# Later adaLN blocks in the first MLP, and attention's small TensorE pieces gathered

## The chip, the cores and the metric

One core of a Trainium2 chip runs the whole program. The metric is the device time of one execution in microseconds (us), median of three runs, lower being better. Five engines take part: TensorE (PE, matrix products and transposes), VectorE (DVE), ScalarE (ACT), GpSimd (POOL) and SyncE (SP, which issues the loads from DRAM). Each runs its own list of instructions in order, and waits where an operand or a buffer is not ready.

## The reference

A trunk of two layers over 256 tokens of width 1024, for one sequence. Layer 0 mixes tokens by a gated convolution, layer 1 by attention with 16 heads of 64; each is followed by an MLP of width 4096. Every sub-layer is modulated (shift, scale, gate) by a vector `c`: that is adaLN, six vectors of 1024 for each layer, each a product of `silu(c)` with a 1024 x 1024 piece of `ada_w`.

```
def reference(x, c, ...):
    cond = silu(c)
    for i in range(2):
        mod = cond @ ada_w[i] + ada_b[i]
        sh1, sc1, g1, sh2, sc2, g2 = split(mod, 6)
        h = rms_norm(x, mix_norm_g[i]) * (1 + sc1) + sh1
        y = conformer_conv(h, ...) if i == 0 else moba_attention(h, w_qkv, q_norm_g, k_norm_g, w_o)
        x = x + g1 * y
        h = rms_norm(x, mlp_norm_g[i]) * (1 + sc2) + sh2
        x = x + g2 * (square(relu(h @ mlp_w1[i])) @ mlp_w2[i])
    return x
```

With 256 tokens there is one key block, so the attention is plain causal attention: q and k are normalised over each head, scores get a slope times the distance, a softmax, and the product with v.

## The kernel before

**Products in three parts.** Every large product is done in fp32 accuracy as three matmuls: weights and activations are each cut into a high and a low part, and `mm3` (L207 to L211) issues high weight by high activation (L208), high weight by low activation (L209), and low weight by high activation (L210), 128 x 128 weights against 258 columns (256 tokens and one column for the shift). A block is 1 MB of weights, 1024 rows by 256 columns; it fills two PSUM banks of 24 matmuls each. The weights come from DRAM into a tile `raw` (five buffers, loaded by SP in the order in which the code asks). `split` (L190 to L203) makes the two parts in two halves: ACT casts the high part `wh` (L196), DVE subtracts for the low part `wl` (L199), and from the fourth block of the first MLP on POOL does a quarter of it (L201). In that MLP a half serves four of the eight matmul triples of both banks, so the third matmul of a bank is the first that needs `wl`.

**The first MLP.** `six` runs the first three w1 blocks (six banks) while the norm's factor is still being made; the factor `rs_ext` (L759, the "seam") is then written and each bank is drained by `evict` (DVE, `tx`, L797), two ACT functions (`s`, `sh`, L833 to L835) and a DVE subtraction (`sl`, L836). The w1 blocks b = 3 to 15 and 16 w2 blocks follow. Beside them, DVE works through adaLN blocks: `ada_dve` loads 1 MB of `ada_w` and issues four DVE operations of 128 x 512 (L299 for the first of a vector, L301 for the others), 24 such blocks in this MLP. `slots` is a list of 32 places: `fill()` takes the next one, three after `six`, one after each block b = 3 to 15, one after each w2 block. The first 8 adaLN blocks ("half 0") are needed first.

**Attention.** For four blocks of four heads (`Heads`, b = 0 to 3) PE's small pieces stand between the triples of the qkv products and, for the last, of the output product `ko`: sums of squares `st`, their transposition `stt`, `kb` (the norm factors of k spread, after DVE's chain from `vs` to `rb`, L961 to L966), `pvt` (v transposed), two `ss` (scores), two `pt` (probabilities transposed), two `po` (product with v). `plan(t)` puts them on a clock that counts the triples issued (`tick`, `at`): the table `ts` gives the offsets in the order squares, stats, norms, keys, values, (scores), (turn), (product). All small pieces take their PSUM from `aux`, three banks in rotation.

**Order.** PE's order is that of the code and the clock. The order of the other engines, and which of two ready instructions stands first, is set when the program is built, by a scheduler that knows `issue_after` (an instruction may be placed only behind the named one). SP's loads go in the order asked, each when a `raw` buffer is free.

Of the kernel before, what the change touches and what calls it, by code (L numbers as in the profile page):

```python
# [30 lines left out]
def trunk(ctx, tc, x, c, ada_w, ada_b, mix_g, mlp_g, w_in, b_in, dw, dw_b, ln_g, ln_b, w_out, b_out,  # L31
# [13 lines left out]
    def aux(name):  # L45
        return axp.tile([P, 512], F32, name=name, tag="ax")
# [4 lines left out]
    def mm_bank(name):  # L51
        return mmp.tile([P, 512], F32, name=name, tag="mm")
# [7 lines left out]
    def at(d, f):  # L60
        later.append((clock[0] + d, f))
# [8 lines left out]
    def drain():  # L70
        while later:
            tick()
# [15 lines left out]
    VEC, cols, box = {}, {}, {}  # L88
# [97 lines left out]
    def load(src, into=None):  # L186
        r = raw() if into is None else into
        box["load"] = sy.dma_start(r, src).ins
        return r

    def split(r, pool_kt=3, parts=1):
        wh = wp.tile([P, 2048], F32R, name="wh")
        wl = wp.tile([P, 2048], F32R, name="wl")
        n = 2048 // parts
        for a in range(0, 2048, n):
            box["cut"] = [act.copy(wh[:, a:a + n], r[:, a:a + n]).ins]  # L196
            m = a + n - 256 * pool_kt
            if m > a:
                box["cut"].append(dve.tensor_sub(wl[:, a:m], r[:, a:m], wh[:, a:m].bitcast(F32)).ins)  # L199
            if pool_kt:  # L200
                pool.tensor_tensor(wl[:, m:a + n], r[:, m:a + n], wh[:, m:a + n].bitcast(F32), op=OP.subtract)  # L201
        return wh, wl

    def kmajor(src):
        return src.rearrange("(k p) n -> p k n", p=P)

    def mm3(ps, wh, wl, ah, al, start, stop, **kw):  # L207
        pe.matmul(ps, wh, ah, start=start, stop=False, **kw)  # L208
        pe.matmul(ps, wh, al, start=False, stop=False, **kw)  # L209
        pe.matmul(ps, wl, ah, start=False, stop=stop, **kw)  # L210
        tick()  # L211
# [247 lines left out]
    half = [b[:, j * S:(j + 1) * S] for b in banks for j in range(2)]  # L459
# [277 lines left out]
    def norm_shift(l, v):  # L737
        sh = mod[:, l, v, :]
        act.copy(xh[:, :, S], sh)
        dve.tensor_sub(xl[:, :, S], sh, xh[:, :, S].bitcast(F32))  # L740
# [55 lines left out]
    def evict(ps, t):  # L796
        box["evict"] = dve.tensor_mul(t, ps[:, :NE], rs_ext).ins  # L797
# [22 lines left out]
    def mlp(l, slots):  # L820

        def fill():
            for f in slots.pop(0) if slots else ():
                f()

        with tc.tile_pool(name=f"mlp{l}", bufs=1) as mp:
            sh = mp.tile([P, FF // P, S], F32R, name="sh")
            sl = mp.tile([P, FF // P, S], F32R, name="sl")
            def finish(ps, f):
                t = mp.tile([P, NE], F32, name="tx", bufs=3)  # L830
                evict(ps, t)
                s = mp.tile([P, S], F32, name="s2", bufs=4)
                act.activation(s, t[:, :S], AF.Relu, bias=t[:, S:S + 1])  # L833
                act.activation(sh[:, f, :], s, AF.Square)
                act.activation(s, s, AF.Square)  # L835
                dve.tensor_sub(sl[:, f, :], s, sh[:, f, :].bitcast(F32))  # L836

            def w1_split(b):
                return split(load(kmajor(w1[l, :, b * 256:(b + 1) * 256])), 1 if l == 0 and b >= 3 else 0, 2)

            six(w1_split, "m1", finish)
            with tc.issue_after(box["evict"]):
                for _ in range(3):
                    fill()
            for b in range(3, FF // 256):
                with tc.issue_after(box["seam"]) if b > 3 else ExitStack():
                    wh, wl = w1_split(b)
                for j in range(2):
                    f = 2 * b + j
                    ps = mm_bank("m1")  # L850
                    for k in range(KT):
                        o = 256 * k + P * j
                        mm3(ps[:, :NE], wh[:, o:o + P], wl[:, o:o + P], xh[:, k, :], xl[:, k, :],
                            start=(k == 0), stop=(k == KT - 1))
                    finish(ps, f)
                fill()
            def put_out(n):
                po = aux("ot")
                for t in range(2):
                    pe.transpose(po[:, t * P:(t + 1) * P], xT[:, n, t * P:(t + 1) * P], ident)  # L860
                o = mp.tile([P, S], F32, name="ot", bufs=2)
                act.copy(o, po[:, :S])
                sy.dma_start(out[0, :, n * P:(n + 1) * P].rearrange("(t p) n -> p t n", p=P),
                             o.rearrange("p (t n) -> p t n", t=2))
            if l == 0:
                acc = work.tile([P, S], F32, name="acc", bufs=2)
            for b in range(D // 256):
                ps = [mm_bank("m2") for _ in range(2)]
                for kc in range(4):
                    wh, wl = split(load(kmajor(w2[l, kc * D:(kc + 1) * D, b * 256:(b + 1) * 256])), 1 if l == 0 else 0, 2)  # L870
                    for j in range(2):
                        for k in range(KT):
                            o = 256 * k + P * j
                            kk = kc * KT + k
                            mm3(ps[j][:, :S], wh[:, o:o + P], wl[:, o:o + P], sh[:, kk, :], sl[:, kk, :],
                                start=(kk == 0), stop=(kk == FF // P - 1))
                        if kc < 3:
                            continue
                        n = 2 * b + j
                        dve.scalar_tensor_tensor(xT[:, n, :], ps[j][:, :S], mod[:, l, 5, n:n + 1],  # L880
                                                 xT[:, n, :], op0=OP.mult, op1=OP.add)
                        if l == 0:
                            norm_prep(1, 0, n, acc)
                        else:
                            at(12, lambda n=n: put_out(n))
                    fill()

            if l == 0:
                norm_shift(1, 0)
                norm_scale()  # L890
            else:
                drain()

    seq = [[(0, 5), (1, 1)], [(1, 0), (1, 2), (1, 4), (1, 3)]]
    slots = [[] for _ in range(32)]
    for half, vs in enumerate(seq):
        fs = [lambda l=l, v=v, q=q: ada_dve(l, v, q) for l, v in vs for q in range(4)]
        for n, f in enumerate(fs):
            slots[(1 if half == 0 else 15) + n * 15 // len(fs)].append(f)
    mlp(0, slots)  # L900


    with tc.tile_pool(name="attn", bufs=1) as ap:
# [14 lines left out]
        class Heads:  # L918
# [3 lines left out]
                self.b, self.tx, self.p, self.pT = b, {}, {}, {}  # L922

            def plan(self, t):
                ts = (2, 5, 11, 24, 26, (30, 40), (52, 70), (60, 78)) if self.b < 3 else (1, 11, 15, 27, 24, (31, 38), (47, 55), (55, 63))
                at(t + ts[0], self.squares)
                at(t + ts[1], self.stats)
                at(t + ts[2], self.norms)
                at(t + ts[3], self.keys)
                at(t + ts[4], self.values)  # L930
                for j in range(2):
                    at(t + ts[5][j], lambda j=j: self.scores(j))
                    at(t + ts[6][j], lambda j=j: self.turn(j))
                    at(t + ts[7][j], lambda j=j: self.product(j))
# [109 lines left out]
        for b in range(4):  # L1044
            hb = Heads(b)

            def take(ps, n):
                t = hb.tx[n // 2, n % 2] = ap.tile([P, NE], F32, name="tqkv", bufs=8)
                evict(ps, t)

            def qkv_split(z):
                return split(load(kmajor(w_qkv[0, :, z * D + b * 256:z * D + (b + 1) * 256])), 0, 2)

            if b == 0:
                six(qkv_split, "qkv", take)
                hb.plan(0)
            for z in range(3 if b == 0 else 0, 3):
                wh, wl = qkv_split(z)
                if z == 2:
                    hb.plan(7 if b < 3 else 0)  # L1060
                for j in range(2):
                    ps = mm_bank("qkv")
                    for k in range(KT):
                        o = 256 * k + P * j
                        mm3(ps[:, :NE], wh[:, o:o + P], wl[:, o:o + P], xh[:, k, :], xl[:, k, :],
                            start=(k == 0), stop=(k == KT - 1))
                    take(ps, 2 * z + j)
# [30 lines left out]
```

## Time and profile before

| | |
|---|---|
| time, median of three runs | 678.72 us (678.38 to 680.17) |
| the profiled execution's own time | 676.28 us |
| its span in the profile | 674.4 us |
| PE busy | 655.1 us, 97% |
| DVE busy | 494.5 us, 73% |
| ACT busy | 369.9 us, 55% |
| POOL busy | 125.3 us, 19% |
| data moved | 150.07 MB |

The span runs from the first to the last recorded instruction; the time has 1.9 us more around it. Matmuls overlap each other, so a busy PE shows rows of some 0.28 us whose starts are 0.12 us apart. In a timeline a row is a run of like instructions: start, length, engine, line, operation, what it writes and reads, shape and count, and in brackets the idle time ahead of it with what ended it. In this execution the first MLP's seam is at 172 us, its w1 blocks end near 257 us, its w2 blocks near 343 us, and attention's small pieces lie between 375 and 476 us.

### The profile page before, as it was taken

The page shows a single profiled execution, that of the slowest core. Times are in us where ns is not written, and L with a number is a line of the kernel's source. Part 1 is how long each engine was busy: PE and PEld are TensorE (multiplying, and loading weights), DVE is VectorE, ACT ScalarE, POOL GpSimd, SP SyncE. Part 2 cuts the span into 40 slices and gives each one's busy share as a digit, 9 for nine tenths or more (in the row PEclk, how much of TensorE's full clock was granted, in tenths as well). Part 3 has the DMA queues.
Part 4 walks back from the last instruction along what each step waited for, and adds up shares of the span by engine and source line. Part 5 has one row for each costly group of instructions (what it writes and reads, how often), then busy time and mean ns, then how long its engine had stood idle before and what let it go on. Part 6 is the DMA issues. An engine that isn't in the chain of part 4 may idle for free.

```text
span 674.4 us, 14400 instructions
## 1 busy us (share of the span) xinstructions
PE 655.1 (97%) x5909; PEld 607.0 (90%) x5909; DVE 494.5 (73%) x924; ACT 369.9 (55%) x678; POOL 125.3 (19%) x167
## 2 busy tenths in 40 slices
PE   7899999999979999999999899999999999999997
PEld 6777865699979999999999888888999999999997
DVE  3647993558999899999964888886878986444440
ACT  4437442485866667254443566575659777533330
POOL 5461042302523424344420000000200000000000
PEclk9999999999979999999999999999999999999999
DMA  8998509675589899999992723433266996555300
GB/s 304 340 351 299 220 8 370 237 252 201 188 275 319 281 302 311 358 340 368 339 322 96 239 75 126 136 119 123 68 197 236 312 304 194 172 189 178 119 18 16
DMA packets 107871, 150.07 MB, mean 223 GB/s; under 512 B 2871, under 2 KB 91120, under 8 KB 107806
## 3 DMA queue, kind: packets, MB, share of 16 engines
q1 hardware_dynamic: 107310, 149.04, 65.8%
q8 instruction: 46, 0.75, 0.4%
q14 instruction: 19, 0.16, 0.1%
q0 software_dynamic: 352, 0.07, 0.1%
q10 hardware_dynamic: 144, 0.06, 0.0%
HBM read 148.10 MB, written 1.05 MB: 221 GB/s over the span
## 4 chain that ended last, share of the span: by engine, by line
PE 86%; DVE 6%; POOL 2%; ACT 2%; DMA 2%; issue 1%; SPq 1%; DVEq 0%; ACTq 0%; POOLq 0%
PE m L208 18%; PE m L210 18%; PE m L209 17%; PE cv L403 3%; PE qkv L208 3%; PE qkv L209 3%; PE qkv L210 3%; PE ci L208 2%; PE ko L208 2%; PE ko L209 2%; PE ko L210 2%; PE rep L393 2%; PE ci L210 2%; PE ci L209 2%; DMA keep<-in_conv_w_in_dram 2%; DVE wl L199 1%
## 5 line engine op out<-in xcount | busy, mean ns | idle before, releaser
L199 DVE TENSOR_TENSOR wl<-raw,wh 128x1024 fp32r<-128x1024 f32 (+2 forms) x176 | 204.8, 1184 | 59.2 <-ACT wh L196 58.2
L196 ACT CAST wh<-raw 128x1024 fp32r<-128x1024 f32 x176 | 177.9, 1044 | 111.6 <-PE m L209 58.1
L210 PE MATMUL m<-xh,wl 128*128 128x258 f32 x512 | 145.4, 284 | 4.2 <-DVE wl L199 4.2
L208 PE MATMUL m<-xh,wh 128*128 128x258 f32 x512 | 146.1, 285 | 0.5 <-DVE xT L789 0.5
L209 PE MATMUL m<-xl,wh 128*128 128x258 f32 x512 | 145.6, 284 | 0.0
L208 PE MATMUL m<-sh,wh 128*128 128x256 f32 x512 | 145.4, 284 | 0.0
L210 PE MATMUL m<-sh,wl 128*128 128x256 f32 x512 | 144.1, 281 | 0.0
L209 PE MATMUL m<-sl,wh 128*128 128x256 f32 x512 | 144.0, 281 | 0.0
L210 PEld LDWEIGHTS m<-xh,wl 128*128 128x128 f32 x512 | 97.8, 191 | 4.4 <-DVE wl L199 4.4
L208 PEld LDWEIGHTS m<-xh,wh 128*128 128x128 f32 x512 | 97.6, 191 | 1.7 <-DVE xT L789 0.9
L208 PEld LDWEIGHTS m<-sh,wh 128*128 128x128 f32 x512 | 96.4, 188 | 1.6 <-issue 1.6
L209 PEld LDWEIGHTS m<-xl,wh 128*128 128x128 f32 x512 | 97.8, 191 | 0.0
L209 PEld LDWEIGHTS m<-sl,wh 128*128 128x128 f32 x512 | 96.4, 188 | 0.0
L210 PEld LDWEIGHTS m<-sh,wl 128*128 128x128 f32 x512 | 96.4, 188 | 0.0
L201 POOL TENSOR_TENSOR wl<-raw,wh 128x256 fp32r<-128x256 f32 (+1 forms) x60 | 68.5, 1153 | 108.6 <-ACT wh L196 106.0
L301 DVE SCALAR_TENSOR_TENSOR ada_a<-raw,cond,ada_a 128x512 f32<-128x512 f32 x98 | 81.2, 860 | 0.6 <-DMA raw<-in_ada_w_dram 0.4
L208 PE MATMUL qkv<-xh,wh 128*128 128x258 f32 x192 | 57.2, 298 | 0.0
L833 ACT ACTIVATE s<-tx 128x256 f32<-128x256 f32 x64 | 31.7, 506 | 41.1 <-DVE tx L797 41.1
L209 PE MATMUL qkv<-xl,wh 128*128 128x258 f32 x192 | 54.3, 283 | 0.0
L210 PE MATMUL qkv<-xh,wl 128*128 128x258 f32 x192 | 54.1, 282 | 0.0
L730 POOL TENSOR_TENSOR acc<-acc,nsq 128x256 f32<-128x256 f32 x15 | 12.8, 851 | 158.0 <-ACT nsq L728 157.4
L208 PEld LDWEIGHTS qkv<-xh,wh 128*128 128x128 f32 x192 | 36.2, 189 | 4.6 <-issue 4.6
(256 smaller groups left out, 1125.1 us busy)
## 6 DMA issues: line engine op xcount, KB each, us to landing
raw<-in_mlp_w_dram SPq DMA_DIRECT2D x64, 1024.0 KB, 6.5
raw<-in_ada_w_dram SPq DMA_DIRECT2D x46, 1024.0 KB, 7.5
raw<-in_attn_w_qkv_dram SPq DMA_DIRECT2D x12, 1024.0 KB, 5.5
keep<-in_conv_w_in_dram SPq DMA_DIRECT2D x8, 512.0 KB, 9.3
raw<-in_conv_w_in_dram SPq DMA_DIRECT2D x8, 512.0 KB, 5.3
raw<-in_conv_w_out_dram SPq DMA_DIRECT2D x4, 1024.0 KB, 8.4
raw<-in_attn_w_o_dram SPq DMA_DIRECT2D x4, 1024.0 KB, 4.9
early<-in_ada_w_dram SPq DMA_DIRECT2D x2, 1024.0 KB
```

Of the source, the lines that this page charges most:

```text
L196: box["cut"] = [act.copy(wh[:, a:a + n], r[:, a:a + n]).ins]
L199: box["cut"].append(dve.tensor_sub(wl[:, a:m], r[:, a:m], wh[:, a:m].bitcast(F32)).ins)
L201: pool.tensor_tensor(wl[:, m:a + n], r[:, m:a + n], wh[:, m:a + n].bitcast(F32), op=OP.subtract)
L208: pe.matmul(ps, wh, ah, start=start, stop=False, **kw)
L209: pe.matmul(ps, wh, al, start=False, stop=False, **kw)
L210: pe.matmul(ps, wl, ah, start=False, stop=stop, **kw)
L301: dve.scalar_tensor_tensor(a, w, cond[:, k, 0:1], a, op0=OP.mult, op1=OP.add)
L393: pe.matmul(ps[32 * r:32 * r + 32, :284], ident[:, 32 * g:32 * g + 32], UT[i][:, r:r + 284], start=True, stop=True, tile_position=(0, 32 * ...
L403: pe.matmul(ps[32 * g:32 * g + 32, :S], W[:, g, q, :], G[:, g, 4 * q:4 * q + S], start=(q == 0), stop=(q == 7), tile_position=(0, 32 * g))
L730: pool.tensor_tensor(acc, acc, q, op=OP.add)
L833: act.activation(s, t[:, :S], AF.Relu, bias=t[:, S:S + 1])
```

## The change

Two parts. The first moves half 0 of the adaLN blocks to later slots: from slots 1, 2, 4, 6, 8, 10, 12, 14 to slots 3, 4, 6, 7, 9, 10, 12, 13, and holds the slots behind blocks b = 3, 4 and 5 back behind the newest `evict`. The second replaces attention's table of offsets: the pieces of all four head blocks get new places. No operation is added or removed.

```diff
@@ mlp: the loop over w1 blocks
                     finish(ps, f)
-                fill()
+                with tc.issue_after(box["evict"]) if b < 6 else ExitStack():
+                    fill()
@@ slots of the first MLP
         for n, f in enumerate(fs):
-            slots[(1 if half == 0 else 15) + n * 15 // len(fs)].append(f)
+            slots[3 + n * 12 // len(fs) if half == 0 else 15 + n * 15 // len(fs)].append(f)
@@ Heads.plan
-                ts = (2, 5, 11, 24, 26, (30, 40), (52, 70), (60, 78)) if self.b < 3 else (1, 11, 15, 27, 24, (31, 38), (47, 55), (55, 63))
+                ts = ((2, 5, 12, 30, 42, (36, 42), (58, 66), (63, 75)),
+                      (9, 12, 18, 31, 47, (37, 47), (60, 79), (66, 85)),
+                      (9, 12, 18, 31, 47, (37, 47), (60, 79), (66, 85)),
+                      (1, 12, 18, 31, 43, (37, 43), (53, 59), (59, 64)))[self.b]
@@ the qkv loop
                 if z == 2:
-                    hb.plan(7 if b < 3 else 0)
+                    hb.plan(0)
```

In triples counted from the end of `six` in attention, the head blocks' clocks start at 0, 39, 87 and 128 before, and at 0, 32, 80 and 128 now. The 40 small pieces stand in 37 separate places between triples before, and in 26 now.

DVE's order from the seam on, before. `tx<-m_2175` drains a bank of the blocks that `six` ran, `tx<-m_2265` the first bank after them, `s_…` are ACT's outputs that `sl` needs, twelve `ada_a` operations in all stand ahead of the `wl` of block b = 5:

```order
L797 TENSOR_TENSOR tx<-m_2175,rs_ext 128x258
L299 TENSOR_SCALAR ada_a<-raw,cond 128x512 x2
L836 TENSOR_TENSOR sl<-s_2216,sh 128x256
L836 TENSOR_TENSOR sl<-s_2223,sh 128x256
L301 SCALAR_TENSOR_TENSOR ada_a<-raw,cond,ada_a 128x512 x2
L836 TENSOR_TENSOR sl<-s_2230,sh 128x256
L836 TENSOR_TENSOR sl<-s_2237,sh 128x256
L301 SCALAR_TENSOR_TENSOR ada_a<-raw,cond,ada_a 128x512 x4
L797 TENSOR_TENSOR tx<-m_2265,rs_ext 128x258
```

Ten rows on, behind four more `ada_a` operations, the two `wl` of block 5 follow. The same place now:

```order
L797 TENSOR_TENSOR tx<-m_2175,rs_ext 128x258
L836 TENSOR_TENSOR sl<-s_2216,sh 128x256
L836 TENSOR_TENSOR sl<-s_2223,sh 128x256
L797 TENSOR_TENSOR tx<-m_2252,rs_ext 128x258
L836 TENSOR_TENSOR sl<-s_2230,sh 128x256
L836 TENSOR_TENSOR sl<-s_2237,sh 128x256
L797 TENSOR_TENSOR tx<-m_2284,rs_ext 128x258
L299 TENSOR_SCALAR ada_a<-raw,cond 128x512 x2
L301 SCALAR_TENSOR_TENSOR ada_a<-raw,cond,ada_a 128x512
L836 TENSOR_TENSOR sl<-s_2279,sh 128x256
L301 SCALAR_TENSOR_TENSOR ada_a<-raw,cond,ada_a 128x512
L199 TENSOR_TENSOR wl<-raw,wh 128x768
```

Four adaLN operations instead of twelve stand ahead of block 5's first `wl`, and none ahead of the drains `tx` of the two banks that follow `six`.

PE's order where the first head block's factors for k are used, before: `kb` and `pvt` stand apart, two triples between them.

```order
L210 MATMUL qkv<-xh,wl 128x258
L986 MATMUL kb<-ident,rb 128x128 x4
L208 MATMUL qkv<-xh,wh 128x258
L209 MATMUL qkv<-xl,wh 128x258
L210 MATMUL qkv<-xh,wl 128x258
L208 MATMUL qkv<-xh,wh 128x258
L209 MATMUL qkv<-xl,wh 128x258
L210 MATMUL qkv<-xh,wl 128x258
L979 MATMUL pvt<-ident,v 128x128 x4
L208 MATMUL qkv<-xh,wh 128x258
```

The place of that `pvt` now, twelve triples behind `kb`:

```order
L210 MATMUL qkv<-xh,wl 128x258
L984 MATMUL pvt<-ident,v 128x128 x4
L1004 MATMUL ss<-k,q 128x128 x2
L1004 MATMUL ss<-k,q 128x256 x2
L208 MATMUL qkv<-xh,wh 128x258
```

`pvt` moved from two triples behind `kb` into one place with the second scores (line numbers in `Heads` are 5 higher now); `kb` itself stands 18 triples behind `stt` instead of 13.

## Rows read from the trace of the kernel before

**Rows 1.** The page, busy time: us, share of the span, instructions.

```profile
PE 655.1 (97%) x5909; PEld 607.0 (90%) x5909; DVE 494.5 (73%) x924; ACT 369.9 (55%) x678; POOL 125.3 (19%) x167
```

**Rows 2.** PE's waits: for what, us in total, times, longest.

```profile
PE m L210 <- DVE wl L199: 4.2, 1, 4.2
PE kb L986 <- DVE rb L966: 2.4, 1, 2.4
...
PE st L951 <- ACT asq L945: 0.4, 1, 0.4
PE pt L1029 <- DVE p L1007: 0.4, 1, 0.4
```

**Rows 3.** PE's timeline, first bank of block 5 in the first MLP.

```profile
186.40 0.28 PE L209 MATMUL m<-xl,wh 128*128 128x258 f32 x1
190.87 0.58 PE L210 MATMUL m<-xh,wl 128*128 128x258 f32 x1 [4.19 <-DVE wl L199]
...
195.77 0.34 PE L208 MATMUL m<-xh,wh 128*128 128x258 f32 x1
```

**Rows 4.** Stretches: us, busy (count) by engine, PE's granted clock, DMA share, GB/s.

```profile
189.00:196.00 7.00, 5.13 (x24) 5.13 (x25) 5.71 (x7) 3.22 (x5) 1.97 (x2) 0.51 0.79 248
...
172.10:257.40 85.30, 81.11 (x662) 80.36 (x662) 80.22 (x128) 58.62 (x114) 29.27 (x27) 0.96 0.87 285
257.40:343.00 85.60, 85.60 (x731) 83.42 (x730) 84.22 (x110) 39.97 (x58) 37.39 (x35) 1.00 1.01 345
376.00:480.00 104.00, 100.45 (x832) 90.15 (x832) 83.61 (x240) 64.21 (x144) 0.00 (x0) 1.00 0.39 128
```

**Rows 5.** DVE's timeline from the seam to block 5's `wl`.

```profile
177.31 0.87 DVE L299 TENSOR_SCALAR ada_a<-raw,cond 128x512 f32<-128x512 f32 x2
...
180.76 4.20 DVE L301 SCALAR_TENSOR_TENSOR ada_a<-raw,cond,ada_a 128x512 f32<-128x512 f32 x4
...
189.21 0.74 DVE L301 SCALAR_TENSOR_TENSOR ada_a<-raw,cond,ada_a 128x512 f32<-128x512 f32 x1
189.87 1.82 DVE L199 TENSOR_TENSOR wl<-raw,wh 128x768 fp32r<-128x768 f32 x2
```

**Rows 6.** DVE's groups in 172.1 to 257.4: busy us, mean ns, idle ahead.

```profile
L301 DVE SCALAR_TENSOR_TENSOR ada_a<-raw,cond,ada_a 128x512 f32<-128x512 f32 x37 | 30.0, 843 | 0.0
L199 DVE TENSOR_TENSOR wl<-raw,wh 128x768 fp32r<-128x768 f32 x26 | 28.4, 1113 | 1.1 <-ACT wh L196 1.1
L836 DVE TENSOR_TENSOR sl<-s,sh 128x256 fp32r<-128x256 f32 x28 | 12.2, 447 | 2.7 <-ACT s L835 2.6
```

**Rows 7.** DVE's and PE's timelines at the seventh w2 block.

```profile
291.61 1.50 DVE L199 TENSOR_TENSOR wl<-raw,wh 128x768 fp32r<-128x768 f32 x1
...
293.85 0.28 PE L208 MATMUL m<-sh,wh 128*128 128x256 f32 x1
```

**Rows 8.** PE's timeline in attention, small pieces and the products beside them.

```profile
403.25 0.87 PE L1038 MATMUL po<-pT,vt 128*64 128x256 f32 x8
...
404.27 0.28 PE L209 MATMUL qkv<-xl,wh 128*128 128x258 f32 x1
...
415.80 0.93 PE L999 MATMUL ss<-k,q 64*128 64x128 f32 x8
...
416.88 0.28 PE L209 MATMUL qkv<-xl,wh 128*128 128x258 f32 x1
...
434.51 0.28 PE L210 MATMUL qkv<-xh,wl 128*128 128x258 f32 x1
434.72 0.87 PE L1038 MATMUL po<-pT,vt 128*64 128x256 f32 x8
...
436.61 0.28 PE L209 MATMUL qkv<-xl,wh 128*128 128x258 f32 x1
```

**Rows 9.** DVE's timeline behind the scores of the second head block.

```profile
414.98 0.18 DVE L1018 RECIPROCAL sm<-sm 128x4 f32<-128x4 f32 x1 [1.58 <-ACT p L1016]
...
416.11 0.42 DVE L1042 TENSOR_TENSOR ol<-po,oh 128x256 fp32r<-128x256 f32 x1
```

## Prediction

> **What bounds the kernel now.** I read the page first. PE is busy in 97% of the span, DVE in 73% [rows 1], so what can be gained lies where PE stops or runs slowly, and the list of PE's waits names those places: 4.2 us for one `wl` in the first MLP, 2.4 us for `rb` in attention, and two of 0.4 [rows 2]. The timeline of the first place shows that the stop costs more than its wait. In the first bank of block 5 the second matmul starts at 186.40 and the third at 190.87, against 0.12 us from start to start elsewhere (81.11 us for 662 matmuls, [rows 4]): 4.35 lost. From 190.87 the 22 starts up to 195.77 take 4.90 instead of 2.64 [rows 3], because the granted clock in 189 to 196 was 0.51, which is the 1.2 GHz level [rows 4]: 2.26 lost. Together 6.6 us. Around the stop of 2.4 in attention the clock stayed at 1.00 (376 to 480, [rows 4]), so the size from which a stop costs the clock as well lies somewhere between 2.4 and 4.2. The reader is to see in DVE's timeline why: from 177.31 to 189.95 twelve adaLN operations run among the drains, and only then, at 189.87, the two `wl` that PE needs [rows 5].
>
> **Part one, the adaLN slots.** Nothing is added; operations change places. Ahead of block 5's first `wl` stand 4 adaLN operations instead of 12. One takes between 0.66 us (189.21 to 189.87, [rows 5]) and 0.76 (the mean of 0.84 less the 0.08 by which such rows overlap, [rows 6]). Eight fewer bring that `wl` forward by 5.3 to 6.1 us. It was done at about 190.8, so now at 184.7 to 185.5, and PE wants it at 186.5. This stop goes, with the half clock behind it: 6.6 us at most, and nothing less unless the same work is late elsewhere.
>
> What is late next is block 8, since the eight adaLN blocks now come closer together. From 180.5, when the second bank behind `six` ends (two banks of 24 matmuls, 5.74 us, before block 5, whose first matmul is one ahead of 186.40, [rows 3]), to 205.2, when PE wants block 8's second `wl` (three such blocks and 14 matmuls behind block 5's start), there are 24.7 us. In that order DVE has 16 adaLN operations, 8 `wl`, 7 `tx` and 8 `sl`. With the shortest rows (0.66, 0.91 for `wl`, [rows 5], 0.37 for the small ones, [rows 6] less the overlap) this is 10.6 + 7.3 + 5.5 = 23.4 us; with the means, less the overlap, 12.2 + 8.3 + 5.5 = 26.0. So DVE is done between 1.3 us before PE wants it and 1.3 after; it also idles for ACT (3.7 us in these 85 us, [rows 6], so 1.1 in 24.7). I take a loss of 1.0, with 0 and 2.4 (1.3 + 1.1) as ends. Behind block 8 a slot without adaLN follows and DVE catches up. **Part one: 6.6 - 1.0 = 5.6 us.** Loads: the first w1 load after `six` now goes ahead of two adaLN loads on SP instead of behind them, which can only bring weights earlier; the adaLN ones later are used later.
>
> PE's gain has to last through the w2 blocks. There DVE is busy 84.22 of 85.60 us [rows 4], and the seventh block's second `wl` is done at 293.11, while PE, which starts the block at 293.85, wants it 14 matmuls later at 295.5 [rows 7]: a margin of 2.4. A PE that is 5.6 earlier keeps its gain only if DVE is earlier too. It can be: it idles 5.1 us in the w1 stage (85.30 less 80.22, [rows 4]), named as waits for PE and for ACT behind PE [rows 6], and these shrink when PE no longer stops. I take it that it comes along.
>
> The Trainium skill, "TensorE: Matmul & The Clock Gate", The HAM clock gate, says that TensorE's clock is throttled by default and that activity releases it. The trace agrees: 0.51 behind the stop of 4.2 us, and full speed again once the matmuls had run for some time. By that page a new long stop would be paid for twice; that case is a rival below, priced from rows.
>
> **Part two, attention.** Three things change.
>
> Old stops go: 2.4 for `kb` and 0.4 each for `st` and `pt` [rows 2], 3.2 us. `kb` stands 5 triples later, 1.8 us, and by DVE's order `rb` has one small operation less ahead of it (0.4, by the small rows of [rows 6]), so of its 2.4 about 0.2 is left.
>
> Pieces are joined: 11 places fewer. A `po` alone takes from 403.25 to 404.27, the second product behind it, 1.02 us; an `ss` alone 1.08; both together 434.72 to 436.61, 1.89 [rows 8]. Apart there is a product of 0.12 more in the sum, and another lead-in of 0.21 (434.51 to 434.72) instead of 0.12: one join saves 2.10 - 1.89 - 0.12 + 0.09 = 0.18. Eleven times that is 2.0; nothing is the other end, as joins of other shapes have no row. I take 1.5, nearer to the row.
>
> The Trainium skill, "TensorEngine Tiling (Array Packing)", Key Properties, says that changing the tiling mode drains the TensorE. The joined pieces are of unlike modes, so by that page a join would save nothing and the sum would be 1.5 us smaller. The row of `po` with `ss`, which are of unlike shapes too, saves 0.18 and does not agree.
>
> New stops come. The three `aux` banks are the cause: `pvt` and two `ss` in one place take all three. In the second head block this place stands 4 triples (1.4 us) behind a `po`, whose bank is free only when DVE has done a reciprocal, four scalings and `ol`, 414.98 to 416.53, 1.55 us [rows 9]. If DVE starts that late by its other work I price 1.0, ends 0 and 2.4 (the longest stop of attention, [rows 2]). The remaining places with a shorter run-up (`kb` of the second and third block, `st` of the last, the second scores of the first, the last `po`) I price together at 1.6, four times the 0.4 of [rows 2], ends 0 and 3. With the 0.2 at `kb`: 2.8. **Part two: 3.2 + 1.5 - 2.8 = 1.9 us**, ends -2.4 (no gain by joining, all new stops at their ends) and 5.0 (joins at 2.0, only the 0.2 left).
>
> **Sum.** 5.6 + 1.9 = 7.5 us. The profiled execution took 676.28 (span 674.4 and 1.9 around it), so 668.8. The median of the three runs, 678.72, stands 2.4 above that execution, and against it the forecast is 671.2. I call 0.3%, 2.0 us, the least that can be told from no change.
>
> **Rivals.**
>
> DVE is the bound of the first MLP. Then the wait only moves on to the w2 blocks and part one is worth the margin of 2.4 [rows 7]. Total 4.3: 674.4. For it: DVE's 84.22 of 85.60 [rows 4]. Against: the 5.1 us of idle time just ahead. 0.18.
>
> Attention gives nothing: joins save little and the `aux` banks stop PE as often as `rb` did. Part two is -1 to 0, total 4.6 to 5.6: 673.1 to 674.1. For it: there are only three banks, and DVE, busy 83.61 of 104 us there [rows 4], is on each chain that a piece waits for. Against: most pieces keep or widen their distance to what they need. 0.12.
>
> The clock falls again. If DVE's list to block 8 runs at rates above the means (four adaLN operations took 4.20 at 180.76, [rows 5]), sixteen of them at 1.05 are 4.6 us more than at 0.76, the stop there is near 5 us, beyond the 4.2 that halved the clock, and part one is worth nothing to 1.2. Total 1.9 to 3.1: 675.6 to 676.8. 0.10.
>
> Slower: each of the four places where `pvt` and `ss` are joined waits for DVE's scalings as long as `kb` did, 2.4 us. That is 9.6 instead of the 1.0 priced, and if the longest of them takes the clock down too, 2.3 more: a total of -3.4, 682.1. The sign turns from four such stops of 2.1 on. Against it: before, what hung on the scores' chain stopped PE for 0.4 only [rows 2]. 0.05.
>
> That the first part does not do what it says is excluded by DVE's order as built. The forecast itself, 667 to 673, has 0.55.
>
> **Range and chances.** 667.0 to 676.5 holds the forecast's case, the two partial ones and half of the clock's; outside are part two at its best (joins at 2.0, no new stops) and the slower case. Faster by over 0.3%, below 676.7: the forecast, the first two rivals and part of the third, 0.85 with a little taken off for what no row shows; same 0.10; slower 0.05.
>
> **What would show it.** Part one: no wait for `wl` of over 2.5 us, no stretch at 0.5 clock behind 186 us; short waits for `wl` at blocks 7 and 8; no such wait in the w2 blocks. If part one fails by the first rival, waits for `wl` will stand at 290 to 300. Part two: the wait of `kb` for `rb` under 0.5 us, waits of `ss` for an earlier `ol` or `p`, and pairs such as `po` with `ss` at 1.9 from start to second product. The prediction would be wrong if the adaLN loads, now asked for later, came late to DVE, for transfers are not priced here beyond their order.

## The result, and the profile after

The changed kernel takes 671.47 us (median of four runs, 670.39 to 673.31) against 678.57 of the kernel before: 0.9896 of it, 95% interval 0.9871 to 0.9920. The profiled execution took 670.39, 5.9 less than that of before.

**Busy time, from the page after** (against [rows 1]):

```profile
PE 654.0 (98%) x5909; PEld 605.2 (91%) x5909; DVE 494.2 (74%) x924; ACT 369.2 (55%) x678; POOL 125.6 (19%) x167
```

The same work on every engine in a shorter span: what went is idle time and slow time of PE. Its waits after (for what, us in total, times, longest), against [rows 2]:

```profile
PE m L210 <- DVE wl L199: 1.8, 3, 0.8
...
PE ko L209 <- DVE ol L1047: 0.9, 1, 0.9
...
PE ss L1004 <- ACT vt L986: 0.3, 1, 0.3
...
PE kb L991 <- DVE ws L974: 0.2, 1, 0.2
```

One stop of 4.2 has become three of at most 0.8, and the wait of 2.4 for `rb` at the first head block's `kb` is gone. (The 0.2 is the second block's `kb`, which waits for `ws` and waited 0.3 before.) New are a wait of 0.9 behind the last `po` and one of 0.3 at an `ss`. PE's timeline after, the three waits for `wl`:

```profile
194.51 0.39 PE L210 MATMUL m<-xh,wl 128*128 128x258 f32 x1 [0.45 <-DVE wl L199]
...
207.30 0.39 PE L210 MATMUL m<-xh,wl 128*128 128x258 f32 x1 [0.62 <-DVE wl L199]
...
338.92 0.38 PE L210 MATMUL m<-sh,wl 128*128 128x256 f32 x1 [0.77 <-DVE wl L199]
```

They lie at blocks 6 and 8 of w1 and in the fifteenth of the 16 w2 blocks. (The w2 products run from 253.5 to 350.1 us here, and before from 257.3 to 353.1, not to 343 as the section on the time before has it.) Stretches after (columns as in [rows 4]):

```profile
189.00:196.00 7.00, 6.55 (x55) 6.34 (x54) 7.00 (x13) 4.75 (x9) 1.79 (x2) 1.00 0.66 204
...
257.40:343.00 85.60, 84.77 (x718) 82.72 (x717) 83.94 (x108) 38.49 (x54) 40.42 (x35) 1.00 1.01 344
```

The granted clock in 189 to 196 is 1.00 instead of 0.51. DVE's timeline after, ahead of block 5's first `wl`:

```profile
181.31 0.87 DVE L299 TENSOR_SCALAR ada_a<-raw,cond 128x512 f32<-128x512 f32 x2
...
183.58 0.74 DVE L301 SCALAR_TENSOR_TENSOR ada_a<-raw,cond,ada_a 128x512 f32<-128x512 f32 x1
184.25 0.95 DVE L199 TENSOR_TENSOR wl<-raw,wh 128x768 fp32r<-128x768 f32 x1
```

That `wl` is done at 185.20, where [rows 5] had it at 190.8.

To divide the gain I use the sums of the three norms (`nss` on PE), which bound the two stages. First the kernel before, then the changed one:

```profile
164.28 0.28 PE L750 MATMUL nss<-onesD,acc 128*128 128x1 f32 x2
...
362.28 0.28 PE L750 MATMUL nss<-onesD,acc 128*128 128x1 f32 x2
...
491.08 0.28 PE L750 MATMUL nss<-onesD,acc 128*128 128x1 f32 x2
```

```profile
164.49 0.28 PE L750 MATMUL nss<-onesD,acc 128*128 128x1 f32 x2
...
359.22 0.28 PE L750 MATMUL nss<-onesD,acc 128*128 128x1 f32 x2
...
485.25 0.28 PE L750 MATMUL nss<-onesD,acc 128*128 128x1 f32 x2
```

From the first to the second lies the first MLP: 198.00 us before, 194.73 after, 3.27 less. From the second to the third lies attention: 128.80 and 126.03, 2.77 less. What follows the third is 183.3 us in both. These stretches are steadier than the whole time, whose start varies from one execution to the next (last section).

### The profile page after: what moved, and what is told of

The parts are those of the page before. It is cut to its first block, busy times and chain, and to the rows that moved or that the text cites. A ratio compares the mean times of both kernels' runs of the same rounds, so it can differ in the third digit from the quotient of the medians.

```text
span 668.6 us, 14398 instructions
## 1 busy us (share of the span) xinstructions
PE 654.0 (98%) x5909; PEld 605.2 (91%) x5909; DVE 494.2 (74%) x924; ACT 369.2 (55%) x678; POOL 125.6 (19%) x167
## 4 chain that ended last, share of the span: by engine, by line
PE 68%; DVE 21%; issue 4%; ACT 3%; POOL 2%; DMA 2%; SPq 1%; DVEq 0%; ACTq 0%; POOLq 0%
PE m L208 11%; PE m L210 11%; PE m L209 11%; DVE ada_a L301 8%; DVE wl L199 7%; PE qkv L208 4%; PE qkv L209 3%; PE qkv L210 3%; PE cv L403 3%; PE ko L209 2%; PE ko L208 2%; PE ci L208 2%; PE ko L210 2%; PE rep L393 2%; PE ci L210 2%
```

## Experiments

All twelve, with the same two stretches read from each profile (the expectations measure attention's from one writing of `rs_ext` to the next, where it is 124.9 in the changed kernel, and e9's figure of 212.2 runs from the first product of the MLP to the second `rs_ext`). "Before" was 678.43 in the runs beside e1 to e4, 678.79 beside e5 to e8, 677.62 beside e9 to e12.

| kernel | median us | ratio to before, 95% | MLP stretch | attention stretch |
|---|---|---|---|---|
| before | 678.57 | | 198.00 | 128.80 |
| changed | 671.47 | 0.9871 to 0.9920 | 194.73 | 126.03 |
| e1 slots only | 673.89 | 0.9928 to 0.9961 | 194.85 | 128.84 |
| e2 table only | 674.67 | 0.9939 to 0.9966 | 197.31 | 126.01 |
| e3 kb later | 677.65 | 0.9975 to 1.0001 | 198.60 | 129.12 |
| e4 apart | 671.04 | 0.9886 to 0.9928 | 194.86 | 126.26 |
| e5 spread | 671.56 | 0.9891 to 0.9934 | 195.37 | 126.11 |
| e6 POOL half | 675.04 | 0.9936 to 0.9969 | 198.51 | 126.11 |
| e7 POOL none | 672.71 | 0.9897 to 0.9946 | 196.28 | 126.05 |
| e8 ko order | 672.10 | 0.9886 to 0.9935 | 195.15 | 125.34 |
| e9 half adaLN | 668.54 | 0.9838 to 0.9893 | 191.40 | 126.04 |
| e10 no hold | 674.17 | 0.9928 to 0.9967 | 196.73 | 126.03 |
| e11 kb early | 672.91, one run | | 194.80 | 127.77 |
| e12 ss late | 674.69, one run | | 194.96 | 128.68 |

Where a kernel leaves a stage as it was, its stretch shows the spread of one execution: 197.3 to 198.6 and 194.7 to 195.2 in the MLP, 126.0 to 126.1 in attention.

**e1 and e2: each part alone.** e1 has the new slots and the hold, with the old table; e2 the new table with the old slots.

> Part one alone: the adaLN slots and the hold of the changed kernel, attention's old table. Theory, from the two profiles: between the norm sums ahead of the first MLP's seam and those behind its end PE needs 3.3 us less than before, so about 675.3 against 678.6, with waits for wl of 0.3 to 0.8 at blocks 7 and 8 and at the end of the w2 blocks, and no stretch at half clock behind 186 us. Rival, by the prediction's sum: 5.6 us, 673.0.

> Part two alone: attention's new table, the adaLN slots as before. Theory, from the two profiles: attention is 2.5 to 2.8 us shorter, so about 676, and the stop of 4.2 us with the half clock behind it stands in the first MLP as before. Rival, by the prediction's sum: 1.9 us, 676.7. Second rival: the parts are not independent (DVE's order in attention hangs on how far its loads are ahead), then the two parts' gains don't add up to the 7.1 of both.

The parts are independent: 3.15 us of the MLP stretch go with the first, 2.79 of attention's with the second, the other stretch stays within its spread. By the medians they are 4.5 and 3.8, and the 95% interval of each holds the figure from the stretches. The MLP stretch with the old stop in it varies most: against before it is 0.69 shorter in e2 and 0.60 longer in e3, nearly all of it in how long the starts behind the stop stay 0.22 apart.

**e3: one stop taken away alone**, in the kernel before.

```diff
-                ts = (2, 5, 11, 24, 26, (30, 40), (52, 70), (60, 78)) if self.b < 3 else
+                ts = (2, 5, 11, 24 if self.b else 30, 26, (30 if self.b else 36, 40 if self.b else 46), (52, 70), (60, 78)) if self.b < 3 else
```

> The kernel before, with one head block's table alone edited: the first kb stands 6 triples later (30 instead of 24), its two scores 6 later too. Theory that the wait for rb is what that place costs: the wait of 2.4 falls to 0.2 to 0.6, gain 1.8 to 2.2, so about 676.6. Rival: what is later stops later (the first turn and product now stand 16 instead of 22 triples behind the first scores), gain under 0.8.

The stop did not go, it went on to the next head block. PE's timeline in e3, there:

```profile
405.98 1.08 PE L986 MATMUL kb<-ident,rb 128*128 128x128 f32 x4 [2.11 <-DVE ws L969]
...
407.07 0.42 PE L209 MATMUL qkv<-xl,wh 128*128 128x258 f32 x1
407.29 0.42 PE L210 MATMUL qkv<-xh,wl 128*128 128x258 f32 x1
```

The second scores of the first head block now stand behind the second block's squares, so on DVE their work stands ahead of the second block's norm chain, and that chain is late. Starts 0.22 apart behind the stop show the lower clock too. The attention stretch is 0.32 longer, not 2 shorter: the rival of the expectation, by another piece than it named.

**e11 and e12: the two entries that matter, put back in the changed table.**

```diff
e11:
-                ts = ((2, 5, 12, 30, 42, (36, 42), (58, 66), (63, 75)),
+                ts = ((2, 5, 12, 24, 42, (36, 42), (58, 66), (63, 75)),
e12:
-                ts = ((2, 5, 12, 30, 42, (36, 42), (58, 66), (63, 75)),
+                ts = ((2, 5, 12, 30, 46, (36, 46), (58, 66), (63, 75)),
```

> The changed kernel with the first head block's kb back at triple 24 instead of 30, nothing else moved. Theory that this place's wait for rb is the old stop of 2.4: it comes back with 1.9 to 2.4, and the stretch between the second and the third norm's sums, 124.9 us, grows to 127. Rival: the new table's order on DVE has rb early enough, under 0.8 more.

> The changed kernel with the first head block's pvt and second scores at triple 46 instead of 42, behind the second block's squares (44) instead of ahead of them. Theory that the stop at the second block's kb hangs on which stands first on DVE, the scores' operations of one head block or the norm chain of the next: that kb waits for ws some 1.5 to 2.1 us, as in the kernel with kb later, and the stretch between the norms' sums grows from 124.9 to 126.5 or more. Rival: 13 triples are enough for the chain either way, under 0.5 more.

PE's waits, e11 first, then e12:

```profile
PE kb L991 <- DVE rb L971: 1.5, 1, 1.5
```

```profile
PE kb L991 <- DVE ws L974: 1.4, 1, 1.4
PE ss L1004 <- ACT sr L959: 0.7, 1, 0.7
PE ss L1004 <- ACT vt L986: 0.5, 1, 0.5
```

In e11 the old stop is back with 1.5 and the attention stretch 1.74 longer. In e12 it is at the second block's `kb`, as in e3, with two smaller ones at `ss`, and the stretch is 2.65 longer, almost the whole gain of part two. So the gain needs both: `kb` later, and the first block's scores done ahead of the second block's squares. In e11 the wait is below the 1.9 to 2.4 expected.

**e4: the joined pieces pulled one triple apart**, 40 places instead of 26.

```diff
-                ts = ((2, 5, 12, 30, 42, (36, 42), (58, 66), (63, 75)),
-                      (9, 12, 18, 31, 47, (37, 47), (60, 79), (66, 85)),
-                      (9, 12, 18, 31, 47, (37, 47), (60, 79), (66, 85)),
-                      (1, 12, 18, 31, 43, (37, 43), (53, 59), (59, 64)))[self.b]
+                ts = ((2, 5, 12, 30, 42, (36, 43), (58, 66), (63, 75)),
+                      (9, 12, 18, 32, 47, (38, 48), (60, 79), (66, 85)),
+                      (9, 13, 19, 32, 47, (38, 48), (60, 79), (66, 85)),
+                      (1, 13, 19, 32, 43, (38, 44), (53, 59), (60, 64)))[self.b]
```

> The changed kernel with every joined pair pulled one triple apart: 40 places instead of 26, almost nothing else moved. Theory that a join saves the lead-in and the way out (0.18 by the row of po with ss): 14 places cost up to 2.5 us, so 673 to 674 against 671.5 of the changed kernel. Rival, the rule that a change of the tiling mode drains the array whatever stands between: 0, 671.5. Second rival: pulled apart, pvt's copy has time to free its bank, and the 0.3 of that stop comes back; then 0.3 less of a loss.

The attention stretch is 0.23 longer and the time 0.4 shorter, which is no change. But stops moved too: `pvt` and `ss` of the second block lose 0.36 less (the 0.3 for `vt` is gone from the list of waits, as the second rival had it), a `st` loses 0.6 less, and the last `pt` waits for `p` and loses 0.7 more. So what a join is worth is read from rows without a stop. PE's timeline of a `pt` and a `st`, joined (changed kernel), then apart (e4):

```profile
415.48 0.82 PE L1034 MATMUL pt<-ident,p 128*128 128x128 f32 x6
416.23 0.64 PE L956 MATMUL st<-asq,hsel 128*32 128x256 f32 x8
...
417.02 0.28 PE L209 MATMUL qkv<-xl,wh 128*128 128x258 f32 x1
```

```profile
415.60 0.82 PE L1034 MATMUL pt<-ident,p 128*128 128x128 f32 x6
...
416.71 0.64 PE L956 MATMUL st<-asq,hsel 128*32 128x256 f32 x8
...
417.50 0.28 PE L209 MATMUL qkv<-xl,wh 128*128 128x258 f32 x1
```

From the first piece to the second product behind the last: 1.54 joined, 1.90 apart, and between the pieces of e4 stand three products, 0.36. The join saves nothing, and neither does that of the first `pvt` with `ss` (1.61 joined; 1.96 apart, with three products between). For `po` with `ss`, joined and apart:

```profile
428.42 0.87 PE L1043 MATMUL po<-pT,vt 128*64 128x256 f32 x8
...
430.31 0.28 PE L209 MATMUL qkv<-xl,wh 128*128 128x258 f32 x1
```

```profile
428.42 0.87 PE L1043 MATMUL po<-pT,vt 128*64 128x256 f32 x8
...
429.77 0.93 PE L1004 MATMUL ss<-k,q 64*128 64x128 f32 x8
...
430.97 0.28 PE L210 MATMUL qkv<-xh,wl 128*128 128x258 f32 x1
```

Joined 1.89; apart 2.55 to one product further (0.12) with three products between (0.36): 2.07, so 0.18 is saved, as in [rows 8]. The difference is in the form of the pieces: `pt` and `pvt` have the products' own form (128*128), `po` (128*64) and `ss` (64*128) have not.

**e5: the slots spread more evenly.**

```diff
-            slots[3 + n * 12 // len(fs) if half == 0 else 15 + n * 15 // len(fs)].append(f)
+            slots[(3, 5, 6, 8, 9, 11, 12, 14)[n] if half == 0 else 15 + n * 15 // len(fs)].append(f)
```

> The changed kernel with the eight adaLN blocks of half 0 in slots 3, 5, 6, 8, 9, 11, 12, 14: 12 instead of 16 adaLN operations are asked for ahead of block 8. Theory that the two stops at blocks 7 and 8 (2.0 us with their ways out) come from the number of adaLN operations ahead of them: they shrink to under 0.5, gain 1.5, 670.0. Rival, DVE is the bound of this MLP: the stops move to later blocks or the last w2 blocks, and the time stays at 671.5. Second rival: by DVE's order all eight operations of two slots stand together ahead of block 8's first wl, so a longer stop stands there, 673 or more.

The rival holds: the waits for `wl` are 2.0 in five places instead of 1.8 in three, later ones (213, 219, 270, 317, 342 us), the MLP stretch is 0.64 longer, and the median is the same.

**e6 and e7: POOL's share of `wl` in blocks 3 to 8**, half, and none.

```diff
e6:
-                ..., 1 if l == 0 and b >= 3 else 0, 2)
+                ..., (2 if b < 9 else 1) if l == 0 and b >= 3 else 0, 2)
e7:
+                ..., 1 if l == 0 and b >= 9 else 0, 2)
```

> The changed kernel, with POOL taking half of wl instead of a quarter in blocks 3 to 8 of the first MLP: DVE's wl are 128x512 there. Theory that DVE's list is what makes PE stop at blocks 7 and 8: 12 wl of some 0.3 less are 3.6 us of DVE, the stops go, gain 1.5 to 2.0, 669.5 to 670. Rival that DVE loses its time to POOL working beside it (rows of DVE beside POOL take up to 1.5 times their shortest): more of POOL's work stretches DVE's other rows, and the stops stay or grow, 671.5 to 674; wl would then come from POOL last.

> The same place the other way: POOL takes no part of wl in blocks 3 to 8, DVE does all of it (128x1024). Theory of DVE's list: 12 wl of 0.25 more, 3 us more work on DVE ahead of block 8, stops longer by 2 to 3 us, 673.5 to 674.5. Rival of DVE beside POOL: DVE's rows there fall to their shortest (0.66 for an adaLN operation), which gives back 2.8 us, and the time stays within 0.7 of the changed kernel's.

DVE's groups in 180 to 208 us, columns as in [rows 6]: the changed kernel, e6, e7.

```profile
L301 DVE SCALAR_TENSOR_TENSOR ada_a<-raw,cond,ada_a 128x512 f32<-128x512 f32 x14 | 11.9, 864 | 0.0
```

```profile
L301 DVE SCALAR_TENSOR_TENSOR ada_a<-raw,cond,ada_a 128x512 f32<-128x512 f32 x13 | 14.0, 1115 | 0.0
```

```profile
L301 DVE SCALAR_TENSOR_TENSOR ada_a<-raw,cond,ada_a 128x512 f32<-128x512 f32 x13 | 9.8, 781 | 0.0
L199 DVE TENSOR_TENSOR wl<-raw,wh 128x1024 fp32r<-128x1024 f32 x7 | 8.5, 1221 | 0.0
```

With more work on POOL one adaLN operation of DVE goes from 864 to 1115 ns, and the MLP stretch is 3.8 longer: e6's first theory is wrong and its rival's mechanism right, though the median of 675.04 lies above the rival's range, and what PE waits for is DVE's `wl`, not POOL's. Without POOL it falls to 781, `wl` grows to 1221, and the stretch is 1.6 longer. Of these, 1.3 are lost in starts 0.22 apart behind a stop of 2.48 (last section). Without them some 0.2 would be left, as the rival had it, though the rows did not fall as far as it had them. So half is worse than a quarter; that a quarter is better than none is not shown, as e7's six runs go from 670.07 to 675.43 and the profile is of the one of 675.43.

**e8: the output product's last weights in another order**, to have `ol` later.

```diff
+            if kp == 3:
+                nj = [(n, 0) for n in range(4)] + [(n, 1) for n in range(4)] + nj[8:]
```

> The changed kernel with the first eight triples of the output product's last weights in another order: four that need the sixth head pair's output ahead of the four that need the last one's ol. The wait of 0.9 for ol behind the last po goes, with its way out 1.0 us: 670.5. Rival: that wait only moves to the first residual sums, which end 1 us later, or hides nothing: 671.5.

Both halves came true. The wait for `ol` is gone and the attention stretch 0.69 shorter; but the same code also makes the first layer's output product, and there the residual comes later. PE's timeline of e8:

```profile
159.19 0.39 PE L208 MATMUL m<-xh,wh 128*128 128x258 f32 x1 [1.09 <-DVE xT L791]
```

The time does not change.

**e9: half of the adaLN work on DVE.** The second of the two terms of each block is left out in the first MLP, and so half of the sum over k in those vectors; all loads stay.

```diff
-            for j in range(2):
+            for j in range(1 if (l, v) != (1, 5) else 2):
```

> The changed kernel without the second of the two terms of each adaLN block in the first MLP: 48 of its 96 adaLN operations of DVE are left out (half of the sum over k is missing in these vectors), all loads stay. Theory that DVE's amount of work is what still stops PE in this MLP: every wait for wl goes, at blocks 7 and 8 and at the last w2 blocks, 3.3 us less between the two norms' sums, 212.2 falls to 209, about 668.2. Rival, the loads (DMA busy 1.01 in the w2 blocks; ACT waits 1.0 us for a load ahead of the last block): the stops at 7 and 8 go, the last one stays or grows as PE comes earlier, 669.5 or more.

```profile
164.88 0.28 PE L750 MATMUL nss<-onesD,acc 128*128 128x1 f32 x2
...
356.28 0.28 PE L750 MATMUL nss<-onesD,acc 128*128 128x1 f32 x2
```

191.40 us, and no wait for `wl` at all in its list of PE's waits. That is 6.60 less than before: the whole of the old stop. The loads, the same as in the changed kernel, do not stop PE there.

**e10: the new slots without the hold.**

```diff
-                with tc.issue_after(box["evict"]) if b < 6 else ExitStack():
-                    fill()
+                fill()
```

> The changed kernel without the hold: the slots behind blocks 3 to 5 no longer wait for the newest evict in DVE's order. As built, eight adaLN operations then stand among the rsqrt steps ahead of rs_ext. Theory that DVE's place in the order decides: rs_ext comes 3 to 6 us later, PE stops for a free bank behind it, 674 to 677. Rival: the first banks behind the seam hide it, and the operations are off the list ahead of block 8, 670 to 671.5.

DVE's timeline of e10 at the norm's factor, and PE's wait for it:

```profile
168.57 0.16 DVE L752 TENSOR_SCALAR nv<-nss 128x2 f32<-128x2 f32 x1 [0.21 <-PE nss L750]
168.65 0.75 DVE L301 SCALAR_TENSOR_TENSOR ada_a<-raw,cond,ada_a 128x512 f32<-128x512 f32 x1
...
177.40 0.42 DVE L759 COPY rs_ext<-nrs 128x256 f32<-128x256 f32 x1 [0.63 <-PE nrs L758]
```

```profile
PE nrs L758 <- DVE rsq_y L180: 2.2, 1, 2.2
```

adaLN operations stand between the small steps of the rsqrt, `rs_ext` comes 8.8 us behind `nv` instead of the changed kernel's 6.4, and PE waits. The MLP stretch is 2.0 longer than with the hold, the time 2.7. The first theory holds, with two corrections: `rs_ext` is 2.4 later and not 3 to 6, and PE waited ahead of the factor's own transposition, not for a bank.

No version tried is faster than the changed kernel by more than the runs differ, but for e9, which computes less (667.40 to 668.83 against 670.39 to 673.31).

## Why the prediction was right, and where its terms were off

The time came out as forecast, in part by luck. Part one gave 3.3 us by its stretch where 5.6 was forecast, part two 2.8 where 1.9 was: errors of opposite sign, which cancel in part, and 6.0 in all where 7.5 was forecast. That the median still came within 0.3 of 671.2 is owed to its 7.1, which is more than the stages show.

**The old stop (6.6).** Right, with its mechanism: with fewer adaLN operations ahead, `wl` was done at 185.2, inside the 184.7 to 185.5 forecast, and the half clock went with the stop. e9 measures the term itself: 6.60. That is the term of this execution; in e2 it is 0.7 less and in e3 0.6 more.

**What is late next (1.0).** Block 8 was right, the size not, and block 6 was not named. The starts at the stops lie 2.0 us further apart than in a run of products, 0.7 at block 6 and 1.3 at block 8: 0.45, 0.13 and 0.62 of waits, the rest on the way in and out of them. DVE's list to block 8 ran near the upper of the two bounds; e6 and e7 show that the length of its rows hangs on POOL's work beside them. I had taken the middle of the bounds.

**"I take it that it comes along."** This step failed. DVE's timeline at the fifteenth w2 block, before, then after:

```profile
337.30 5.18 DVE L199 TENSOR_TENSOR wl<-raw,wh 128x768 fp32r<-128x768 f32 x4
```

```profile
337.38 1.48 DVE L199 TENSOR_TENSOR wl<-raw,wh 128x768 fp32r<-128x768 f32 x1
```

The first `wl` of that block starts at the same time in both, though PE comes to the block at 337.75 instead of 341.83. From the seam to there DVE does the same operations. It idles 4.5 us instead of 6.2, as I had taken it, but the operations take 1.5 longer. In the w2 blocks of the changed kernel it is busy 83.94 of 85.60 us. So PE's lead was not held whole, and 1.35 us were given back in the eleventh and the fifteenth w2 blocks (waits of 0.06 and 0.77 and their ways out). So part one is 6.6 - 2.0 - 1.35 = 3.25, which is what the stretch shows. The first rival, DVE as the bound, had the right mechanism and too high a price: 2.4 was left by its reckoning, 3.3 was. That it is DVE and not the loads is shown by e9; that the number of adaLN operations ahead of one block is not the cause, by e5.

**Old stops in attention (3.2).** Mis-sized: the starts around the stopped pieces give 5.0 us (2.6 and 0.5 at `kb`, 0.6 at `pt`, 1.0 at `pt` with `st`, 0.2 at the last `kb`), since a wait has its way out, and some were waits between the matmuls of one piece that the list of waits does not name. Of the 2.4 for `rb` nothing is left, where 0.2 was forecast. Another 0.6, a wait for the residual ahead of the second MLP, went without my having seen it.

**Joins (1.5).** This term failed: by e4's rows only `po` with `ss` saves 0.18, and there is one such place more than before; pieces of the products' own form save nothing, or 0.05 (`po` with `stt`, two places). About 0.3 in all by the rows. The Trainium skill, "TensorEngine Tiling (Array Packing)", Key Properties, has a change of tiling mode drain the array. I had read it as against the row, and the row as against it. With e4 they agree: between `po` and `ss` without products there is one change fewer, between `pt` and `st` there is not, since `pt` has the products' form.

**New stops (2.8).** 3.3 by the rows: 0.15 at the second block's `kb`, 0.7 at the `pvt` and `ss` of the second block (forecast 1.0), 0.6 and 0.2 at later joined pieces, 0.4 and 1.3 at the last two `po`. The sum was near, and the largest was one that I had put among the small ones. The stop at `pvt` and `ss` had another cause than the one I gave:

```profile
409.87 0.92 PE L1004 MATMUL ss<-k,q 64*128 64x128 f32 x6 [0.26 <-ACT vt L986]
410.07 0.42 DVE L1047 TENSOR_TENSOR ol<-po,oh 128x256 fp32r<-128x256 f32 x1
```

`ss` waited for ACT's copy of `pvt`, and DVE's `ol`, for which I had it wait, started only behind it. With 5.0 and 0.6 gone, 0.3 from joins and 3.3 new, part two is 2.6 by these rows, 2.8 by its stretch.

**The order of pieces.** The prediction took `kb`'s stop as a matter of distance. e3, e11 and e12 show that distance alone only moves it: what counts is whose work stands first on DVE.

The difference between 5.9 (profiles) and 7.1 (medians) is not explained by the stages; single executions of one program differ by as much (below).

## What to carry to other kernels

When the engine that is late is busy nearly all the time, moving its work removes a long stop but leaves the sum: halve its work once, as in e9, to see how much the order can give at all. Price a stop by the starts around it, not by its wait, and a join by the forms of the pieces. In a table of places, check what a moved piece does to the order on the other engines, because a wait taken away at one head block can return at the next.

## What the runs showed of the hardware

**A stop's length does not decide alone whether the clock falls.** The prediction set the border between 2.4 and 4.2 us. But the stop of 2.1 in e3 and that of 2.2 in e10 were followed by starts 0.22 apart, the 1.2 GHz level (granted clock 0.50 in 405.7 to 409.1 and 0.53 in 177.0 to 180.6), where the 2.4 of [rows 2] and one of 2.3 in e6 were not (1.00 in 376 to 480 and in 205 to 216). What else decides, no run here shows. In e7 PE stopped 2.48 us, ran at full pace for about 1 us and only then slowed:

```profile
210.67 0.39 PE L210 MATMUL m<-xh,wl 128*128 128x258 f32 x1 [2.48 <-DVE wl L199]
210.90 0.29 PE L208 MATMUL m<-xh,wh 128*128 128x258 f32 x1
...
212.09 0.42 PE L208 MATMUL m<-xh,wh 128*128 128x258 f32 x1
212.31 0.42 PE L209 MATMUL m<-xl,wh 128*128 128x258 f32 x1
```

**One program, two clocks at its start.** Near 20 us, in a part that no edit touched, PE waits 1.0 to 2.9 us, and in seven of the 14 profiles the clock falls there. Again the length does not decide: it fell at 1.40 (e6) and not at 2.39 (e11). e5's timeline and stretch, then the changed kernel's stretch, where the wait was 1.0:

```profile
20.33 1.01 PE L241 MATMUL adac<-ones,ada_s 128*128 128x1 f32 x4 [2.31 <-ACT ada_s L236]
```

```profile
20.00:30.00 10.00, 9.67 (x63) 8.96 (x64) 4.38 (x12) 1.48 (x6) 3.79 (x2) 0.66 1.07 365
```

```profile
20.00:30.00 10.00, 9.45 (x86) 8.74 (x87) 5.69 (x17) 4.39 (x8) 4.51 (x3) 1.00 1.07 364
```

The runs of the kernel before go in steps with their mean granted clock: 676.5 to 677.5 us at 0.994 or 0.995, 677.7 to 679.7 at 0.992, 679.8 to 680.5 at 0.990. So an edit worth 1 us is seen in a stretch of the profile, and not in a median of a few runs.
